# A hybrid decoder trunk on one core: the gathering tile's residual kept in the PEER accumulators, and 38 resident weight units in place of 31

## The chip, the core and the metric

One core of one Trainium2 chip runs the whole program: TensorE (PE), VectorE (DVE), ScalarE (ACT), GpSimd (POOL), SyncE (SP) and the core's 16 DMA engines. The metric is device microseconds (us) from the start to the end of the program, lower is better. Everything is float32.

## What is computed

The input is 256 tokens of 1024 numbers. Four layers follow each other: HGRN2, FoX attention, Mamba-2 SSD, HGRN2 again. In each, a token mixer and then a PEER layer are added to the residual; a last RMSNorm ends it. Cut to what matters here:

```python
for i in range(DEPTH):                       # 4 layers
    hn = rmsnorm(h, norm_mix[i])
    h = h + mixer[i % 3](hn, ...)            # hgrn2, fox, ssd
    ffn = peer_ffn(rmsnorm(h, norm_ffn[i]), peer_w_q[i], peer_keys[i], peer_u[i], peer_v[i])
    h = h + ffn
return rmsnorm(h, norm_final)

def peer_ffn(...):                           # 8 heads, 16384 experts of one neuron each
    q = (xb @ w_q).reshape(M, 8, 2, 128)
    s = einsum('mhcd,hckd->mhck', q, sub_keys)
    # top 16 of each half, top 16 of their 256 sums -> idx, gates
    u, v = take(u_tab, idx), take(v_tab, idx)
    act = gelu(einsum('md,mhkd->mhk', xb, u)) * gates
    return einsum('mhk,mhkd->md', act, v)
```

## The kernel before

**Tiles and stages.** The tokens are two tiles of 128. Layer and tile together make eight stages, s = 2 * layer + tile (`t`). In stage s the PEER experts of that stage are gathered while, as side work, the next stage's mixer, its second norm and its PEER queries are computed (`side`, L1332, calls `ready(s + 1, ...)`, L1302). Before the first stage the first tile's mixer runs alone (`lone`).

**The gather loop.** A stage has 64 steps (the loop at L1393). A step fetches two blocks of 128 rows of the expert table, one row of 8 KB (u and v) to each partition, so 1024 KB per fetch, by an indirect DMA that POOL issues (`fetch`, L1260). Eight buffers GB hold them, so up to eight fetches are out. DVE multiplies u with the tokens (`dot`, L1271), ACT makes gelu and gate and a diagonal weight (`spread`), and PE adds v times that weight to two PSUM accumulators `acc` (L1296), four products a step. A buffer is free for the next fetch when PE has read it. The accumulators are one pair of PSUM banks, reused by every stage.

**Residual.** Both tiles' residuals lie in SBUF, `h[:, t]`. When a stage's accumulators are complete, the first step of the next stage adds them to `h[:, t]` (`normed(..., alone=True)`, L444: two adds on DVE). Then come squares on ACT, root, scale, and the turned rows go into `xT`.

**Weights.** All weights come in units of 1024 KB, [128, 2048], in a fixed order (`stream`), once for each tile: a layer has 20 to 32 mixer units and 8 of the PEER queries. SP issues the loads (`loads`, L312). Most units pass through a ring of three (`raw`). A layer's first `EARLY` and last `LATE` units have a place of their own in the area `mix`; the second tile finds them there and loads nothing for them (L337). Before, that is 4 + 4 units for either HGRN2, 4 + 3 for FoX and 4 + 4 for SSD: 31 in all. What the mixer itself needs lies between (`middle`) or in the late units' places while the first tile runs, and in the early units' places while the second runs (`outer`). For the very first tile the list `order` (L296) writes out by hand which unit is loaded when, some of them into gather buffers that are still empty (`homes`).

**What sets the order.** Each engine runs its instructions in program order. The side work is cut into slots (`Plan`), and `products_` takes the next slot when its estimated cost so far is below a quota for the stage (`SIDE`, L40). SP's queue is in order too: a load that waits holds back all loads behind it. POOL's queue holds the gathers and four fills of a scratch tile.

Of the kernel before, what the change touches and what calls it, by code (L numbers as in the profile page):

```python
# [10 lines left out]
F32 = mybir.dt.float32  # L11
# [8 lines left out]
P = 128  # L20
# [90 lines left out]
def _layout(x, norm_mix, norm_ffn, norm_final, hgrn_lb_logits, hgrn_w_in, hgrn_gnorm, hgrn_w_out,  # L111
# [21 lines left out]
    def small(m):  # L133
# [5 lines left out]
    a["gn"] = np.ascontiguousarray(hgrn_gnorm)  # L139
    parts = [  # L140
        ("wf", small(w[:, 3072:3088])), ("wdt", small(w2[:, 6144:6176])),
# [24 lines left out]
def trunk(ctx: ExitStack, tc: tile.TileContext, d: dict, out: bass.AP):  # L166
# [15 lines left out]
    sizes = (("h", 2 * D), ("xT", D), ("XR", 2 * D), ("keys", UNIT), ("SS", 2048), ("mix", MIX),  # L182
# [6 lines left out]
    h = at_["h"].rearrange("p (t n) -> p t n", t=2)  # L189
# [56 lines left out]

    def middle(kind):
# [64 lines left out]
    def loads():  # L312

        while order:
# [4 lines left out]
            elif u == "x":  # L319
                nc.sync.dma_start(h[:, 1], d["x"][1])  # L320
# [123 lines left out]
    def normed(t, acc, row, xn, alone=False):  # L444
# [3 lines left out]
        r = st[:, 2:3]  # L448

        def add(e):  # L450
            tm(h[:, t, es[e]], acc[e], h[:, t, es[e]], op=OP.add)

        def square(e):
            act(xn[:, es[e]], h[:, t, es[e]], AF.Square, accum_out=st[:, e:e + 1])
# [5 lines left out]
        def scale():  # L460
            vec.reciprocal(r, r)
            for e in range(2):
                if last and t and e:
                    act(xn[:, es[e]], row[:, es[e]], AF.Copy, scale=r)
                elif last and t:
                    vec.tensor_scalar(xn[:, es[e]], row[:, es[e]], r, None, op0=OP.mult)
                elif last:
                    stt(xn[:, es[e]], h[:, t, es[e]], r, row[:, es[e]], op0=OP.mult, op1=OP.mult)
                if last:
                    nc.sync.dma_start(out[t * P:(t + 1) * P, es[e]], xn[:, es[e]])  # L470
                else:
                    vec.tensor_scalar(xn[:, es[e]], h[:, t, es[e]], r, None, op0=OP.mult)
# [5 lines left out]
        last = not isinstance(row, int)  # L478
        both = [lambda e=e: square(e) for e in range(2)]
        if acc is not None:  # L480
# [3 lines left out]
            else:  # L484
                both = [adds[0], both[0], adds[1], both[1]]
                if last and t:

                    for e in range(2):
                        both.insert(2 + 3 * e, lambda e=e: tm(row[:, es[e]], h[:, t, es[e]], row[:, es[e]], op=OP.mult))
                if lone[0] or last and t:  # L490
# [950 lines left out]
```

## Time and profile before

| what | us |
|---|---|
| median of 3 timed runs | 3188.8 (3187.67 to 3189.03) |
| the profiled execution, whole | 3185.7 |
| its span, first to last instruction | 3183.9 |
| PE busy in the span | 2470.2 (78%) |
| DVE busy | 2115.5 (66%) |
| ACT busy | 1351.3 (42%) |
| POOL busy | 1189.5 (37%) |
| time of the packets of the gathers' queue, as a share of 16 DMA engines | 81.8% |
| the same of the queue that loads weights | 17.3% |
| moved by DMA | 1303.02 MB |

The profile lists one execution. Its page has the busy time of each engine, the span in 40 slices, the DMA queues, and the costliest groups of instructions with the idle time ahead of them and what ended it. The trace behind it can be asked for any stretch of time. A float32 product stands in it as two records of PE. MB are millions of bytes.

### The profile page before, as it was taken

To read this page: it belongs to the slowest core of one execution; us is meant where nothing else is said; L and a number is where in the kernel's file an instruction comes from. 1 tells how busy PE (TensorE), PEld (TensorE's weight loads), DVE (VectorE), ACT (ScalarE), POOL (GpSimd) and SP (SyncE) were. 2 spreads that over 40 slices of the span, in tenths; PEclk is the share of its full clock that TensorE was granted. 3 is DMA by queue.
4 is the path that set the end of the run, shared out by engine and by line. 5 is a ranking of instruction groups with operands and counts; after the bars stand their busy time and mean duration, and the time that the engine had idled before them with its cause. 6 is when DMAs were issued, how large, how long until landed. Compare 5 with 4: busy or idle time off the path is not lost.

```text
span 3183.9 us, 30834 instructions
## 1 busy us (share of the span) xinstructions
PE 2470.2 (78%) x8610; PEld 1095.2 (34%) x8610; DVE 2115.5 (66%) x5584; ACT 1351.3 (42%) x3895; POOL 1189.5 (37%) x1032
## 2 busy tenths in 40 slices
PE   9888787877787876889878898778876877865655
PEld 4433333332333423344333443333332333332222
DVE  2576657675676756878567786476666767676764
ACT  3354324353344523577334773244433543333332
POOL 0243334343343424433334333244433433344443
PEclk9999898988899988999989998989988999898787
DMA  7899999999999999999999999999999999999997
GB/s 299 339 420 421 421 421 419 421 407 421 407 420 421 407 422 414 404 421 421 417 417 401 421 419 415 416 403 410 421 421 421 401 421 421 421 414 421 415 417 330
DMA packets 180025, 1303.02 MB, mean 409 GB/s; under 512 B 19984, under 2 KB 20368, under 8 KB 21520
## 3 DMA queue, kind: packets, MB, share of 16 engines
q0 software_dynamic: 147456, 1073.81, 81.8%
q1 hardware_dynamic: 32400, 227.24, 17.3%
q8 instruction: 72, 1.18, 0.2%
q14 instruction: 97, 0.79, 0.1%
HBM read 1299.92 MB, written 1.05 MB: 409 GB/s over the span
## 4 chain that ended last, share of the span: by engine, by line
DMA 58%; PE 14%; DVE 11%; issue 9%; ACT 4%; POOL 3%; POOLq 0%; DVEq 0%; ACTq 0%
DMA arena<-in_uv,ix 58%; DVE arena L204 8%; PE acc L1296 7%; PE pj L239 5%; POOL arena L1260 3%; PE ps L239 2%; ACT dots L217 1%; ACT L217 1%; DVE cs L204 1%; ACT dg L217 1%; PE ps L243 0%; DVE si L204 0%; ACT arena L217 0%; DVE sv L204 0%; DVE af L204 0%
## 5 line engine op out<-in xcount | busy, mean ns | idle before, releaser
L1260 POOL DMA_INDIRECT arena<-in_uv,ix x1024 | 1185.4, 1158 | 1968.6 <-PE acc L1296 1411.0
L204 DVE SCALAR_TENSOR_TENSOR arena<-arena 128x1024 f32<-128x1024 f32 (+3 forms) x1282 | 1322.1, 1048 | 878.5 <-DMA arena<-in_uv,ix 834.9
L1296 PE MATMUL acc<-arena,dg 128*64 128x512 f32 x4096 | 1285.2, 714 | 693.9 <-ACT dg L217 693.2
L1296 PEld LDWEIGHTS acc<-arena,dg 128*64 128x64 f32 x4096 | 466.0, 152 | 1326.4 <-ACT dg L217 1004.2
L217 ACT ACTIVATE dots<-dots 128x2 f32<-128x2 f32 x512 | 103.2, 202 | 1549.4 <-DVE arena L204 1549.3
L239 PE MATMUL pj<-raw,arena 128*128 128x512 f32 (+1 forms) x1368 | 635.5, 607 | 3.8 <-DMA raw<-in_ssm 2.8
L217 ACT ACT_TABLE_LOAD x325 | 417.0, 1283 | 6.8 <-DVE arena L204 0.8
L239 PEld LDWEIGHTS pj<-raw,arena 128*128 128x128 f32 x1368 | 249.8, 193 | 393.6 <-issue 377.4
L217 ACT ACTIVATE dg<-m,dots 128x64 f32<-128x64 f32 x1024 | 292.5, 333 | 0.0
L239 PE MATMUL pj<-arena 128*128 128x512 f32 x568 | 267.4, 616 | 0.3 <-DVE arena L204 0.3
L217 ACT ACTIVATE dots<-dots,gs 128x1 f32<-128x1 f32 x1024 | 245.6, 287 | 16.7
L239 PEld LDWEIGHTS pj<-arena 128*128 128x128 f32 x568 | 106.4, 197 | 162.5 <-issue 153.2
L239 PE MATMUL ps<-arena 128*128 128x128 f32 (+3 forms) x992 | 129.5, 286 | 1.1 <-ACT arena L1125 0.9
L239 PEld LDWEIGHTS ps<-arena 128*128 128x128 f32 (+2 forms) x992 | 102.7, 167 | 65.3 <-issue 39.0
L243 PEld LDWEIGHTS ps<-fst,arena 128*128 128x128 f32 x568 | 67.3, 147 | 85.5 <-issue 39.9
L243 PE MATMUL ps<-fst,arena 128*128 128x128 f32 x568 | 90.9, 288 | 4.5 <-ACT arena L1124 2.5
L217 ACT ACTIVATE arena<-arena 128x512 f32<-128x512 f32 (+3 forms) x132 | 67.7, 555 | 42.0 <-DVE arena L204 39.5
L204 DVE DVE_READ_ACCUMULATOR arena<-arena 128x1 f32 x1024 | 85.0, 83 | 0.0
L204 DVE FIND_INDEX8 si<-sv,arena 128x8 uint32<-128x128 f32 x256 | 69.9, 286 | 0.0
L239 PE MATMUL ps<-cst,arena 128*128 128x128 f32 (+3 forms) x288 | 67.0, 360 | 0.0
L204 DVE MAX8 sv<-arena 128x8 f32<-128x128 f32 x256 | 61.8, 283 | 5.7 <-ACT arena L1129 5.7
L217 ACT ACTIVATE arena<-ps 128x512 f32<-128x512 f32 (+3 forms) x114 | 43.7, 425 | 29.7 <-PE ps L239 29.0
(116 smaller groups left out, 1248.9 us busy)
## 6 DMA issues: line engine op xcount, KB each, us to landing
raw<-in_hg SPq DMA_DIRECT2D x57, 1024.0 KB, 9.4
raw<-in_ssm SPq DMA_DIRECT2D x56, 1024.0 KB, 9.4
raw<-in_wq SPq DMA_DIRECT2D x32, 1024.0 KB, 9.2
raw<-in_fox SPq DMA_DIRECT2D x24, 1024.0 KB, 9.2
arena<-in_wq SPq DMA_DIRECT2D x17, 1024.0 KB, 16.7
arena<-in_uv,ix POOLq DMA_INDIRECT x1024, 14.9
arena<-in_hg SPq DMA_DIRECT2D x15, 1024.0 KB, 14.1
arena<-in_keys SPq DMA_DIRECT2D x4, 1024.0 KB, 9.3
```

The lines of the kernel that those rows point to most:

```text
L204: return getattr(nc.vector, name)(o, *a, **k)
L217: nc.scalar.activation(o, i, f, **k)
L239: nc.tensor.matmul(o, w, m, start=start, stop=stop)
L243: nc.tensor.transpose(o, i, ident)
L1260: nc.gpsimd.indirect_dma_start(GB[n % NGB], None, d["uv"], bass.IndirectOffsetOnAxis(ap=got[s, hh][0][:, g, q:q + 1], axis=0))
L1296: nc.tensor.matmul(accs[s][e][g * 64:g * 64 + 64], dg[:, g], v, start=hh == 0 and q == 0, stop=hh == 7 and q == NQ - 1)
```

## The change

The residual of the tile whose experts are being gathered goes into that stage's accumulators. Its buffer is scratch from then on, and seven more weight units have places of their own.

- Two buffers `HB` of 1048 columns take the place of `h` (2 x 1024). In a stage one of them holds the residual that the side work works on (`hidden`), the other is its scratch (`spare_of`): the normed rows, HGRN2's `K`, SSD's convolution blocks and the PEER queries, which lay in `middle` before. They swap from stage to stage.
- `begin(s)` opens a stage's accumulators with two products of the identity and the tile's residual; the experts are then added to it. So when the stage ends the accumulators hold the new residual, and `normed(..., alone=True)` copies them out, one half on ACT and one on DVE, where it added both on DVE. The last norm of the second tile reads the accumulators themselves.
- `EARLY` and `LATE` become 5 + 5 for HGRN2, 4 + 5 for FoX and 4 + 5 for SSD: 10 + 9 + 9 + 10 = 38 units. HGRN2's `LF` and `SG`, and halves of FoX's keys and values, move into places of units (`outer`).
- In the hand-written order unit 23 has no gather buffer any more but its late place, and is loaded after the step "heads". The second tile's input is loaded after `begin(0)`, into the buffer that the first tile's residual has left.
- The projections `wf` and `wdt` (128 KB each) are loaded when their layer begins, not with the parameters. FoX's second tile multiplies with its two halves of keys in two products of 128 columns, not one of 256.
- The descriptor area of the gathers, `dynamic_dma_scratch_size`, goes from 4096 to 2048 bytes.

```diff
-EARLY = {"hg": 4, "fox": 4, "ssd": 4}
-LATE = {"hg": 4, "fox": 3, "ssd": 4}
-MIDDLE = {"hg": 4 * D + P, "fox": 64 + 8 * T + 3 * D + P, "ssd": 64 + 192 + 32 + 2 * D + 96 + T + 512 + 8 * 131}
+EARLY = {"hg": 5, "fox": 4, "ssd": 4}
+LATE = {"hg": 5, "fox": 5, "ssd": 5}
+MIDDLE = {"hg": D + P, "fox": 64 + 2 * D + P + T, "ssd": 64 + 192 + 32 + 2 * D + 96 + T + T}
+TURN = 8 * 131
...
-    sizes = (("h", 2 * D), ("xT", D), ("XR", 2 * D), ("keys", UNIT), ("SS", 2048), ("mix", MIX),
+    sizes = (("h0", TURN), ("h1", TURN), ("xT", D), ("XR", 2 * D), ("keys", UNIT), ("SS", 2048), ("mix", MIX),
...
+    def hidden(s):
+        return HB[(s - 1) % 2 if s else 0][:, 0:D]
+    def spare_of(s):
+        return HB[s % 2 if s else 1]
...
-    homes = {7: GB[0], 8: GB[1], 9: GB[2], 10: GB[3], 17: GB[0], 18: GB[1], 19: GB[2], 22: GB[5], 23: GB[6]}
-    order = [0, 1, 2, "rest", 3, 4, 5, 6, 7, 8, 9, 10, 11, 22, 12, 13, 23, 14, "x", 15, 16, 17, 20, 18, 21, 19, "keys",
-             "factors", 24, 25, "heads", 26, "states", 27]
+    homes = {7: GB[0], 8: GB[1], 9: GB[2], 10: GB[3], 17: GB[0], 18: GB[1], 19: GB[2], 22: GB[5]}
+    order = [0, 1, 2, "rest", 3, 4, 5, 6, 7, 8, 9, 10, 11, 22, 12, 13, 14, 15, 16, 17, 20, 18, 21, 19, "keys",
+             "factors", 24, 25, "heads", 23, 26, "states", 27]
...
-    def normed(t, acc, row, xn, alone=False):
+    def normed(h, t, acc, row, xn, alone=False):
...
+        src = [acc[e] if last and t else h[:, es[e]] for e in range(2)]
         def add(e):
-            tm(h[:, t, es[e]], acc[e], h[:, t, es[e]], op=OP.add)
+            if not alone:
+                tm(h[:, es[e]], acc[e], h[:, es[e]], op=OP.add)
+            elif e:
+                vec.tensor_copy(h[:, es[e]], acc[e])
+            else:
+                nc.scalar.copy(h[:, es[e]], acc[e])
...
+        if last and t:
+            for e in range(2):
+                both.insert(1 + 2 * e, lambda e=e: tm(row[:, es[e]], src[e], row[:, es[e]], op=OP.mult))
+            both.insert(2, lambda: act(spare, eps, AF.Sqrt))
...
-                mm(b[:, 0:nk * P], QT[ps, j], KT[ps, j, 0:nk * P], False, True)
+                for s in range(nk):
+                    mm(b[:, s * P:(s + 1) * P], QT[ps, j], KT[s][ps, j], False, s == nk - 1)
...
+    def begin(s):
+        accs[s] = [accp.tile([P, 512], F32, name="acc") for _ in range(2)]
+        for e in range(2):
+            nc.tensor.matmul(accs[s][e], ident, hidden(s)[:, e * 512:(e + 1) * 512], start=True, stop=False)
...
-        if hh == 0 and q == 0:
-            accs[s] = [accp.tile([P, 512], F32, name="acc") for _ in range(2)]
+        if s and hh == 0 and q == 0:
+            begin(s)
...
-                nc.tensor.matmul(accs[s][e][g * 64:g * 64 + 64], dg[:, g], v, start=hh == 0 and q == 0,
+                nc.tensor.matmul(accs[s][e][g * 64:g * 64 + 64], dg[:, g], v, start=False,
...
+        if not t and KIND[l] != "hg":
+            name = {"fox": "wf", "ssd": "wdt"}[KIND[l]]
+            nc.sync.dma_start(middle(KIND[l])(T), d[name])
...
     next(first)
+    begin(0)
+    nc.sync.dma_start(hidden(1), d["x"][1])
...
-    nc = bacc.Bacc("TRN2", target_bir_lowering=False, num_devices=1, dynamic_dma_scratch_size=4096)
+    nc = bacc.Bacc("TRN2", target_bir_lowering=False, num_devices=1, dynamic_dma_scratch_size=2048)
```

**SP, the loads from the first layer's second tile to the end of FoX's.** A row is a run of like loads. `raw` is the ring, `arena` a place of a unit (or a small table); `in_hg` and `in_fox` are mixer weights, `in_wq` those of the PEER queries. Before:

```order
L338 DMA raw<-in_hg 128x2048 x16
L338 DMA raw<-in_wq 128x2048 x4
L338 DMA arena<-in_fox 128x2048 x4
L338 DMA raw<-in_fox 128x2048 x3
L1309 DMA arena<-in_keys 128x2048
L338 DMA raw<-in_fox 128x2048 x9
L338 DMA raw<-in_wq 128x2048 x5
L338 DMA arena<-in_wq 128x2048 x3
L338 DMA raw<-in_fox 128x2048 x12
L338 DMA raw<-in_wq 128x2048 x5
```

After, where one more `raw<-in_hg` stands just ahead of the first row:

```order
L1388 DMA arena<-in_x 128x1024
L345 DMA raw<-in_hg 128x2048 x14
L345 DMA raw<-in_wq 128x2048 x3
L345 DMA arena<-in_fox 128x2048 x4
L345 DMA raw<-in_fox 128x2048 x3
L1329 DMA arena<-in_wf 128x256
L1332 DMA arena<-in_keys 128x2048
L345 DMA raw<-in_fox 128x2048 x9
L345 DMA raw<-in_wq 128x2048 x3
L345 DMA arena<-in_wq 128x2048 x5
L345 DMA raw<-in_fox 128x2048 x12
L345 DMA raw<-in_wq 128x2048 x3
```

The second tile of HGRN2 has 18 loads where it had 20, that of FoX 15 where it had 17. SSD's has 31 where it had 32, and the last HGRN2's 18 where it had 20. The second input tile's load stands behind the first of the second tile's ring loads; before, it stood among the first tile's units, ahead of its unit 15.

**PE, the seam between the first two stages.** `acc<-arena,dg` are the experts' products, four a step; `ps<-fst,arena 64x128` the 32 that repeat the next stage's tokens; `acc<-arena,fst` the products of `begin`. Before:

```order
L1296 MATMUL acc<-arena,dg 64x512 x28
L239 MATMUL ps<-fst,arena 64x128 x32
L1296 MATMUL acc<-arena,dg 64x512 x20
L243 MATMUL ps<-fst,arena 128x128 x8
L1296 MATMUL acc<-arena,dg 64x512 x4
```

After:

```order
L1316 MATMUL acc<-arena,dg 64x512 x28
L240 MATMUL ps<-fst,arena 64x128 x32
L1316 MATMUL acc<-arena,dg 64x512 x4
L1298 MATMUL acc<-arena,fst 128x512 x2
L1316 MATMUL acc<-arena,dg 64x512 x16
L244 MATMUL ps<-fst,arena 128x128 x8
L1316 MATMUL acc<-arena,dg 64x512 x4
```

The two products of `begin` come between the last step of the old stage and the first of the new. The same two stand at each of the seven seams, and once more at the start, behind the 32 repeating products of the first stage.

**DVE, the same seam.** `arena,dots<-arena` are the dots, two a step; `arena<-ps` copies repeated tokens. Before:

```order
L204 SCALAR_TENSOR_TENSOR arena,dots<-arena 128x1024 x4
L204 COPY arena<-ps 128x512
L204 SCALAR_TENSOR_TENSOR arena,dots<-arena 128x1024
L204 TENSOR_TENSOR arena<-acc,arena 128x512 x2
L204 SCALAR_TENSOR_TENSOR arena,dots<-arena 128x1024
L204 MAX sv<-arena 128x8 x2
```

After:

```order
L205 SCALAR_TENSOR_TENSOR arena,dots<-arena 128x1024 x4
L205 COPY arena<-ps 128x512
L205 SCALAR_TENSOR_TENSOR arena,dots<-arena 128x1024
L205 COPY arena<-acc 128x512
L205 SCALAR_TENSOR_TENSOR arena,dots<-arena 128x1024
L205 MAX sv<-arena 128x8 x2
```

Between the two dots of the new stage's first step stands one copy in place of two adds; the other half's copy stands on ACT, ahead of that step's gelu.

## Rows read from the trace of the kernel before

**Rows 1.** The page's second part, the span in 40 equal slices of 79.6 us: the busy share of the DMA engines in tenths, and what they moved.

```profile
DMA  7899999999999999999999999999999999999997
GB/s 299 339 420 421 421 421 419 421 407 421 407 420 421 407 422 414 404 421 421 417 417 401 421 419 415 416 403 410 421 421 421 401 421 421 421 414 421 415 417 330
```

**Rows 2.** Busy time of the engines in stretches: the lone start, the first PEER steps, and the eight gather stages (each from the first product into its accumulators to that of the next). Columns: stretch, its length, busy us and instructions of PE, its weight loads, DVE, ACT and POOL, PE's mean granted clock (1.00 is the higher of its two levels), the busy share of the DMA engines, GB/s.

```profile
0.00:117.00 117.00, 110.22 (x428) 59.47 (x428) 32.77 (x93) 37.81 (x71) 1.16 (x5) 1.00 0.78 306
117.00:160.00 43.00, 38.93 (x130) 18.44 (x130) 28.35 (x86) 15.64 (x45) 20.28 (x17) 0.93 0.90 355
134.00:518.00 384.00, 307.52 (x1057) 131.96 (x1057) 254.89 (x670) 157.81 (x461) 150.58 (x129) 0.92 1.01 416
518.00:892.00 374.00, 281.65 (x976) 123.04 (x976) 248.81 (x673) 149.92 (x471) 145.02 (x128) 0.87 1.01 415
892.00:1272.00 380.00, 287.90 (x1056) 131.55 (x1056) 253.81 (x677) 156.91 (x476) 148.01 (x129) 0.91 1.01 417
1272.00:1687.00 415.00, 345.59 (x1242) 157.36 (x1242) 299.14 (x821) 216.57 (x573) 152.00 (x128) 0.93 1.01 416
1687.00:2104.00 417.00, 346.31 (x1266) 158.23 (x1266) 298.43 (x811) 210.95 (x562) 146.89 (x129) 0.93 1.01 415
2104.00:2489.00 385.00, 296.37 (x1020) 128.15 (x1020) 253.57 (x655) 160.05 (x463) 153.44 (x130) 0.90 1.01 415
2489.00:2855.00 366.00, 289.42 (x1016) 124.68 (x1016) 253.98 (x655) 158.68 (x459) 150.28 (x130) 0.93 1.01 415
2855.00:3158.00 303.00, 177.41 (x482) 69.03 (x484) 200.82 (x492) 91.68 (x338) 133.86 (x121) 0.81 1.01 418
```

**Rows 3.** The page's fifth part, its costliest groups: busy us and mean ns of one, then the idle time before them and what ended most of it. The first is the gather's issue on POOL, the second the projections whose weights come through the ring.

```profile
L1260 POOL DMA_INDIRECT arena<-in_uv,ix x1024 | 1185.4, 1158 | 1968.6 <-PE acc L1296 1411.0
...
L239 PE MATMUL pj<-raw,arena 128*128 128x512 f32 (+1 forms) x1368 | 635.5, 607 | 3.8 <-DMA raw<-in_ssm 2.8
```

**Rows 4.** The page's third and sixth parts: the two DMA queues that carry data (packets, MB, share of the 16 engines' span), and two kinds of DMA issue (count, KB each, median us from issue to landing).

```profile
q0 software_dynamic: 147456, 1073.81, 81.8%
q1 hardware_dynamic: 32400, 227.24, 17.3%
...
raw<-in_hg SPq DMA_DIRECT2D x57, 1024.0 KB, 9.4
...
arena<-in_uv,ix POOLq DMA_INDIRECT x1024, 14.9
```

**Rows 5.** The seam between the first and second stage, instructions in order of time (start, us, engine, line, operation, idle before it and its releaser).

```profile
512.51 2.17 PE L1296 MATMUL acc<-arena,dg 128*64 128x512 f32 x8
...
514.51 1.28 DVE L204 TENSOR_TENSOR arena<-acc,arena 128x512 f32<-128x512 f32 x2
...
515.71 1.22 DVE L204 SCALAR_TENSOR_TENSOR arena<-arena 128x1024 f32<-128x1024 f32 x1
...
516.97 0.20 ACT L217 ACTIVATE dots<-dots 128x2 f32<-128x2 f32 x1 [3.80 <-DVE arena L204]
...
517.98 3.56 PE L1296 MATMUL acc<-arena,dg 128*64 128x512 f32 x8 [3.30 <-ACT dg L217]
```

**Rows 6.** Busy time of the engines in 25 us around the first of the seven seams and the three with the lowest rate, columns as in rows 2.

```profile
508.00:533.00 25.00, 15.79 (x103) 8.43 (x100) 18.39 (x52) 11.56 (x36) 11.50 (x11) 0.85 1.01 419
...
1262.00:1287.00 25.00, 15.90 (x107) 8.86 (x105) 19.00 (x56) 12.82 (x37) 12.60 (x10) 0.91 1.01 413
1677.00:1702.00 25.00, 15.97 (x105) 9.90 (x103) 19.90 (x56) 13.77 (x40) 12.06 (x10) 0.91 0.99 399
2094.00:2119.00 25.00, 16.77 (x107) 9.20 (x106) 19.30 (x56) 11.98 (x37) 11.88 (x11) 0.86 1.00 403
```

**Rows 7.** The start, instructions in order of time, from three pieces of the timeline put one after the other (the first is the warming of PE, three products in the code and six records in the trace).

```profile
1.49 5.37 PE L1278 MATMUL acc<-arena 128*128 128x512 f32 x6 [1.49 <-DVE arena L1345]
...
8.48 14.00 PE L239 MATMUL pj<-arena 128*128 128x512 f32 x32 [0.35 <-DVE arena L204]
...
62.00 0.43 SPq L320 DMA_DIRECT2D arena<-in_x  x1
...
98.73 11.75 SPq L338 DMA_DIRECT2D raw<-in_hg  x3
...
110.06 3.71 PE L239 MATMUL ps<-fst,arena 128*64 128x128 f32 x64
...
115.86 0.69 PE L243 MATMUL ps<-fst,arena 128*128 128x128 f32 x2 [2.09 <-ACT arena L1124]
...
117.16 1.08 POOL L1260 DMA_INDIRECT arena<-in_uv,ix  x1 [115.47 <-DVE ig L204]
...
118.03 12.78 PE L239 MATMUL pj<-arena 128*128 128x512 f32 x24
...
123.12 1.23 DVE L204 SCALAR_TENSOR_TENSOR arena<-arena 128x1024 f32<-128x1024 f32 x1 [5.40 <-DMA arena<-in_uv,ix]
...
134.23 2.17 PE L1296 MATMUL acc<-arena,dg 128*64 128x512 f32 x8 [3.00 <-ACT dg L217]
```

**Rows 8.** The end, instructions in order of time.

```profile
3173.88 1.94 PE L1296 MATMUL acc<-arena,dg 128*64 128x512 f32 x8
...
3175.03 0.69 DVE L204 TENSOR_TENSOR arena<-acc,arena 128x512 f32<-128x512 f32 x1 [3.33 <-PE acc L1296]
3175.75 0.63 ACT L217 ACTIVATE arena<-arena 128x512 f32<-128x512 f32 x1 [2.82 <-DVE arena L204]
```

More of the change, by code (lines that the diff above doesn't have):

```diff
@@ L448, in normed @@
         r = st[:, 2:3]
+        last = not isinstance(row, int)
+        src = [acc[e] if last and t else h[:, es[e]] for e in range(2)]
         def add(e):
-            tm(h[:, t, es[e]], acc[e], h[:, t, es[e]], op=OP.add)
+            if not alone:
[4 more added lines that the diff above has]
+                nc.scalar.copy(h[:, es[e]], acc[e])
         def square(e):
-            act(xn[:, es[e]], h[:, t, es[e]], AF.Square, accum_out=st[:, e:e + 1])
+            act(xn[:, es[e]], src[e], AF.Square, accum_out=st[:, e:e + 1])
         def root():
@@ L467, in scale @@
                 elif last:
-                    stt(xn[:, es[e]], h[:, t, es[e]], r, row[:, es[e]], op0=OP.mult, op1=OP.mult)
+                    stt(xn[:, es[e]], h[:, es[e]], r, row[:, es[e]], op0=OP.mult, op1=OP.mult)
                 if last:
@@ L476, in weighed @@
             tm(xT[:, c], b, weights[:, 8 * row + 4 * q:8 * row + 4 * q + 4].unsqueeze(2).to_broadcast([P, 4, P]), op=OP.mult)
-        last = not isinstance(row, int)
         both = [lambda e=e: square(e) for e in range(2)]
-        if acc is not None:
+        if last and t:
+            for e in range(2):
+                both.insert(1 + 2 * e, lambda e=e: tm(row[:, es[e]], src[e], row[:, es[e]], op=OP.mult))
+            both.insert(2, lambda: act(spare, eps, AF.Sqrt))
+        elif acc is not None:
             adds = [lambda e=e: add(e) for e in range(2)]
@@ L485, in normed @@
                 both = [adds[0], both[0], adds[1], both[1]]
[L486 to L490, printed above, removed]
+                if lone[0]:
                     both.insert(2, lambda: act(spare, eps, AF.Sqrt))
@@ L501, in hgrn @@
         al = middle("hg")
-        K, LF, SG, S = (al(D) for _ in range(4))
-        gn = al(P)
+        K, S, gn = carry["xn"], al(D), al(P)
+        al = outer("hg", t)
+        LF, SG = al(D), al(D)
         QT = SG.rearrange("p (h t) -> p h t", h=8)
@@ L741, in fox @@
         al = middle("fox")
-        al(D)
+        wf = al(T)
         LF = al(64).rearrange("p (t n) -> p t n", t=2)
-        KT = al(8 * T).rearrange("p (b t) -> p b t", b=8)
-        V = al(2 * D).rearrange("p (t n) -> p t n", t=2)
+        KT, V = [al(D)], [al(D)]
         gmem = al(P)
         al = outer("fox", t)
+        if t:
+            V.append(al(D))
+            KT.append(al(D))
+        KT = [k.rearrange("p (b t) -> p b t", b=8) for k in KT]
         QT = al(8 * P).rearrange("p (b t) -> p b t", b=8)
@@ L753, in fox @@
         nk = 1 + t
-        own = slice(t * P, (t + 1) * P)
         ub, sts, acc = {}, {}, []
@@ L776, in keys_turn @@
         def keys_turn(g):
-            turned(TM[1], lambda b: nc.scalar.copy(KT[:, 4 * g:4 * g + 4, own], b))
+            turned(TM[1], lambda b: nc.scalar.copy(KT[t][:, 4 * g:4 * g + 4], b))
         def scores(j):
@@ L887, in steps @@
             stt(DA, DT, -1.0, ea, op0=OP.mult, op1=OP.mult)
-        gate = small_proj("wdt", "dtb", steps, RR)
+        gate = small_proj(wdt, "dtb", steps, RR)
         def suffix():
@@ L1094, in queries @@
         ub = {}
-        al = middle(KIND[l])
-        QB = al(512)
-        QT = al(512).rearrange("p (g t) -> p g t", g=4)
+        QB = spare_of(s)[:, 0:512]
+        QT = spare_of(s)[:, 512:D].rearrange("p (g t) -> p g t", g=4)
         def evac(g):
@@ L1314, in ready @@
             free(("late", l))
-        norm = normed(t, carry["acc"], DEPTH + l, xn)
+        norm = normed(h, t, carry["acc"], DEPTH + l, xn)
         if lone[0]:
@@ L1423, in trunk @@
             pass
-    for _ in normed(1, accs.pop(STAGES - 1), mix[:, 0:D], mix[:, 2 * D:3 * D]):
+    for _ in normed(None, 1, accs.pop(STAGES - 1), mix[:, 0:D], mix[:, 2 * D:3 * D]):
         pass
```

36 lines of the change are left out of this document (16 added, 20 removed).

## The prediction

> **What bounds the kernel now.** I read the slices of the span first. From the third slice to the last but one the DMA engines are at 9 tenths and move 401 to 422 GB/s; only the first two slices (299 and 339) and the last (330) are well below [rows 1]. That is a ceiling, not chance: the eight stages run at 415 to 418 GB/s whatever they compute [rows 2]. The stage from 1687 has 417 us and the one from 2489 has 366 us, both at 415 GB/s, so 173.1 MB and 151.9 MB: 51 us for 21.2 MB, 2.41 us for each MB. The time of a stage is its bytes. The compute engines follow: PE is busy for 307.52 of 384 us in the first stage (80%) and 346.31 of 417 in the fullest (83%), and even there the rate is 415 [rows 2].
>
> Then I read who waits. POOL's idle time ahead of a gather mostly ends with PE's products, which free the buffer [rows 3]; but a gather takes 14.9 us from issue to landing [rows 4], and at 421 GB/s its 1.049 MB is 2.49 us of transfer, so some six gathers' worth of data is ahead of it: the DMA engines have work in reserve while POOL waits. PE waits for ring weights 3.8 us in all [rows 3], so the loads are no latency problem; they cost bytes in the DMA engines. Their queue has 17.3% of the engines' time, the gathers' 81.8% [rows 4].
>
> The start is another regime. Until the first gather (117.16) PE is busy 110.22 of 117 us at 306 GB/s, and until 160 us the rate is 355 [rows 2, 7]. There bytes are free and PE's chain counts.
>
> **The change part by part.** *Seven loads fewer.* The order of SP shows them: two each in the second tile of HGRN2, FoX and the last HGRN2, one in SSD's. 7 x 1024 KB are 7.34 MB. At the ceiling of 421 GB/s [rows 1] that is 17.4 us; by the stages' mean of 416 it is 17.6; by packet time, 99.1% of 3183.9 us for 1301.05 MB, 2.425 us each MB, 17.8 [rows 4]. I take 17.4. All seven are loads of stages that run close to the ceiling (those from 134, 892, 1687 and 2489). One would be a ring load from about 100 us, in the slow start, but the ring stays three loads deep, so the load that disappears is the last of the row, not the first.
>
> The Trainium skill speaks against that price: its page "DMA: Bandwidth & Descriptors", section "Where 436 GB/s comes from", has HBM bind transfers to the core at about 358 GB/s, by which the saving would be an estimated 20.5 us. The trace disagrees: 420 GB/s and more stand in slice after slice [rows 1]. The 17.4 holds without it.
>
> *Small tables.* `wf` and `wdt`, 131 KB each, leave the start and go into the saturated part: 0.262 MB, +0.6 us. They are needed behind the next tile's norm and 1024 KB loads land in 9.4 us [rows 4], so I cost no wait.
>
> *The second input tile* (0.524 MB) was issued at 62.00, and now behind `begin(0)` [rows 7]. SP holds the ring loads behind it, two of 1.049 MB, which were issued by 110.5 and now go at about 115.5. So 2.6 MB move to the first gathers, up to 6.2 us of transfer. But from 117 to 160 us the rate is 355, which leaves 43 us x 66 GB/s = 2.8 MB unused [rows 2], because the queries' products hold PE for 12.78 us from 118.03 and the first expert product comes at 134.23, while its first dot could start at 123.12 [rows 7]. I take 0; if half of the room is already spoken for, +3 us.
>
> *begin.* One such product is two records of 0.44 us (14.00 / 32), or 0.90 in the slowest row (5.37 / 6) [rows 7]: two products are 1.75 to 3.6 us. At the start they fall into PE's gap of 2.09 us ahead of 115.86 [rows 7]: 0. At a seam PE has finished the old stage at 514.68 and waits 3.30 us for ACT until 517.98 [rows 5]. The accumulators come free while it waits: DVE's two adds (1.28 us from 514.51) become one copy on DVE, taken as half of that, and one on ACT, which has nothing else until 516.97. The first product can start at about 514.7, the second at 515.3, and both end by 516.5. DVE's next dot starts 0.6 us earlier, so the chain of dot, gelu and product gains 0.6 us at each of seven seams, if PE keeps up. Around the seams the rate is 399 to 419 [rows 6], the reserve feeds the DMA engines through most of it; I take 0, with 4 us (7 x 0.6) as the gain at best.
>
> *The other PE work.* Eight begins are 14 us of 2470 and FoX's 16 additional products some 14 more at the same price; PE would be busy 82% of a shortened first stage, still under the 83% that runs at 415 [rows 2]. Cover: 18% idle PE. 0.
>
> *The end.* Behind the last product an add (0.69 us, 3175.03) stood ahead of the first square (3175.75) on the path to the output [rows 8]. The square now reads the accumulators: -0.7 us.
>
> *The smaller descriptor area* costs nothing as long as POOL need not wait for an old gather; the trace has no row for that, bounds below.
>
> Sum: -17.4 + 0.6 - 0.7 = -17.5 us. The profiled execution had 3185.7 (a span of 3183.9 and 1.8 around it), which makes 3168.2; its own time was 3.1 under the median, and against the median, 3188.8, I expect **3171.3 us**. From the bounds: +3 at the start and a fifth of the saving lost to steps in which PE is late give 3178; -0.4, 4 at the seams give 3167.
>
> **The rivals.** *Saved bytes, but an engine takes the bound.* If the four shortened stages hung on PE for half of what they save, 8.7 us come back: 3180.0. For it: PE is busy for 80% there, and the rate dips to 401 to 407 in single slices. Against it: the stage from 2855 has next to no weights, so its gathers come faster than they ever will elsewhere, and it runs at 418; the fullest stage still has 415 [rows 2].
>
> *The seams get longer.* If both products wait for the end of both reads and PE runs them at the slow price, they go from about 515.8 to 519.4, 1.4 us past 517.98 [rows 5, 7]; seven times 1.4 is 9.8, and the time is 3181. It would need an empty reserve, too; the poorest seam has 399 GB/s, the first 419 [rows 6].
>
> *Slower: the descriptor area throttles the gathers.* With room for too few, POOL would wait for an old gather to land before it can write the next. The one gather with nothing ahead took 5.96 us, 117.16 to 123.12 [rows 7]; with two at a time that is 2.98 us each, 0.49 above 2.49, and 1024 gathers lose 502 us. With three to five at a time the rate holds on average, but without a reserve each stage would run like the poorest seam, 399 for 416 GB/s [rows 2, 6]: 4.3% of the 3041 us from 134 to 3175, +130 us, so 3301. It decides from fewer than six at a time, the number that the landing time shows. Against it: with the area of before POOL's issues average 1158 ns, and what it waits for is PE [rows 3]; nothing hints that it is near its limit.
>
> On this rival the Trainium skill, "DMA: Bandwidth & Descriptors", sections "Terms" and "The descriptor swizzle", has descriptors of 16 bytes and nine to an engine for a 1 MiB transfer; an estimate from that page is 2048 / 16 = 128, or 14 gathers, more than the eight buffers ask for. The nine agree with the trace, 147456 packets / 1024 gathers / 16 engines [rows 4]; the area's room no run here shows.
>
> That the loads don't go away is no rival: they are gone from SP's order.
>
> **How the numbers follow.** My forecast, 3171.3 with its own range 3167 to 3178, gets 0.82; an engine that takes the bound (about 3180) 0.08; longer seams (about 3181) 0.06; the throttle 0.04. The range is 3165 to 3180: the forecast's with 2 us at the lower end for clock and order effects on the start's chain, and half of the first rival's; 0.14 is left out. A measurement of this kernel tells about 0.2% from no change, 6.4 us, so faster means under 3182.4. The forecast, three quarters of the first rival and two thirds of the second are faster: 0.92. Same: 0.04. Slower: the throttle, 0.04.
>
> **What would show it.** The weights' queue carries about 7.3 MB less, and the stages from 134, 892 and 2489 are some 5 us shorter, the one from 1687 some 2, at the same 415 to 418 GB/s; the other four keep their length. PE's wait ahead of a stage's first expert product shrinks by the 1.75 us of `begin`, and that product does not come later after the seam's last dot. The first gather is still issued at about 117, and the last square starts with no add ahead of it. If the shortened stages show a lower rate at the old length, the first rival holds; if POOL's idle time ends with DMA, or its issues get longer, the third does. I am wrong altogether if PE's chain in the start moves by more than a few us, because there every microsecond counts fully.

## The result, and the profile after

The changed kernel takes 3170.4 us (median of 5 runs, 3169.8 to 3174.4), the kernel before, beside it, 3187.7 (3186.3 to 3189.0): a ratio of 0.9949, 95% interval 0.9935 to 0.9964, or 17.3 us less. The forecast was 17.5 us less and 3171.3. The profiled execution's span is 3172.0, 3173.7 with what lies around it.

The page's second and third parts after: busy share of the DMA engines and GB/s in 40 slices, now of 79.3 us, and the two queues (packets, MB, share).

```profile
DMA  6899999999999999999999999999999999999998
GB/s 271 359 417 421 421 421 422 421 416 422 412 411 421 393 421 413 417 420 419 421 411 407 421 421 407 411 411 409 421 421 399 406 422 421 400 418 421 420 417 337
...
q0 software_dynamic: 147456, 1073.81, 82.2%
q1 hardware_dynamic: 31680, 219.90, 16.8%
```

The ceiling is the one of [rows 1], the gathers' queue is the one of [rows 4], and the weights' queue carries 227.24 - 219.90 = 7.34 MB less: the seven loads. The two small tables have gone from the start into the same queue and don't change its sum.

The stretches that answer to [rows 2], columns as there:

```profile
0.00:118.00 118.00, 111.33 (x432) 60.02 (x432) 32.53 (x92) 37.80 (x71) 1.15 (x5) 1.00 0.69 279
118.00:160.00 42.00, 37.48 (x120) 16.97 (x120) 25.21 (x74) 15.75 (x45) 16.73 (x16) 0.92 1.01 416
133.00:515.00 382.00, 304.64 (x1060) 130.42 (x1060) 258.97 (x684) 158.75 (x461) 153.41 (x129) 0.93 1.01 420
515.00:889.00 374.00, 277.44 (x980) 122.94 (x980) 247.03 (x670) 150.93 (x472) 140.00 (x128) 0.89 1.01 418
889.00:1265.00 376.00, 286.55 (x1093) 130.11 (x1094) 253.25 (x680) 158.74 (x478) 146.31 (x129) 0.90 1.00 412
1265.00:1678.00 413.00, 340.91 (x1248) 154.73 (x1247) 299.31 (x822) 217.91 (x574) 146.89 (x128) 0.94 1.01 418
1678.00:2097.00 419.00, 348.30 (x1270) 158.72 (x1268) 297.98 (x807) 211.65 (x561) 146.38 (x128) 0.91 1.01 414
2097.00:2481.00 384.00, 296.48 (x1024) 127.79 (x1024) 252.83 (x652) 160.26 (x464) 150.07 (x130) 0.90 1.00 412
2481.00:2845.00 364.00, 291.02 (x1020) 124.15 (x1020) 252.73 (x652) 158.76 (x459) 148.27 (x129) 0.92 1.01 413
2845.00:3147.00 302.00, 177.52 (x481) 68.53 (x481) 201.32 (x491) 93.32 (x341) 130.43 (x120) 0.80 1.01 420
```

Read length times rate, not length alone. The stages still run at 412 to 420 GB/s. Their MB, before and after: first 384 x 416 = 159.7 and 382 x 420 = 160.4; third 158.5 and 154.9; fourth 172.6 and 172.6; fifth 173.1 and 173.5; sixth 159.8 and 158.2; seventh 151.9 and 150.3. So the first stage keeps its bytes. The first two rows tell why: the start carried 117 x 306 = 35.8 MB and now 118 x 279 = 32.9; the 42 us behind it run at 416 and carry 17.5 MB where 43 us at 355 carried 15.3. By the queues' packets the first stage's weights do fall, from 26.2 to 24.25 MB, but 2.6 MB more of gathers land in it, since only 3.6 MB of them were moved ahead of its first product, 6.1 before.

The groups that answer to [rows 3], busy us and mean ns, then the idle time ahead:

```profile
L1274 POOL DMA_INDIRECT arena<-in_uv,ix x1024 | 1167.4, 1140 | 1976.1 <-PE acc L1316 1352.9
...
L240 PE MATMUL pj<-raw,arena 128*128 128x512 f32 (+1 forms) x1264 | 586.3, 606 | 3.1 <-DVE arena L205 2.1
```

POOL's issue is no longer than before (1140 ns, 1158 then), what it waits for is still PE, and PE hardly waits for ring weights.

The first seam after, in order of time, which answers to [rows 5]:

```profile
510.00 2.17 PE L1316 MATMUL acc<-arena,dg 128*64 128x512 f32 x8
...
511.34 0.58 ACT L465 COPY arena<-acc 128x512 f32<-128x512 f32 x1 [0.69 <-PE acc L1316]
...
512.09 1.98 PE L1298 MATMUL acc<-arena,fst 128*128 128x512 f32 x4
...
512.20 0.69 DVE L205 COPY arena<-acc 128x512 f32<-128x512 f32 x1
512.81 1.22 DVE L205 SCALAR_TENSOR_TENSOR arena<-arena 128x1024 f32<-128x1024 f32 x1
...
515.07 2.17 PE L1316 MATMUL acc<-arena,dg 128*64 128x512 f32 x8 [0.99 <-ACT dg L218]
```

The products of `begin` wait for the copies and lie where PE waited 3.30 us before; 0.99 is left. The new stage's first expert product comes 1.04 us after the end of the seam's last dot (512.81 + 1.22 = 514.03), as before (1.05, from 516.93 to 517.98). From the old stage's last product to that first one it is 2.90 us, 3.30 before.

### The profile page after: what moved, and what is told of

It reads as the page before. It is cut to its first block, busy times and chain, and to the rows that moved or that the text cites. A ratio compares the mean times of both kernels' runs of the same rounds, so it can differ in the third digit from the quotient of the medians.

```text
span 3172.0 us, 30948 instructions
## 1 busy us (share of the span) xinstructions
PE 2458.5 (78%) x8674; PEld 1088.0 (34%) x8674; DVE 2110.0 (67%) x5575; ACT 1359.4 (43%) x3904; POOL 1171.5 (37%) x1032
## 3 DMA queue, kind: packets, MB, share of 16 engines
q1 hardware_dynamic: 31680, 219.90, 16.8%
HBM read 1292.58 MB, written 1.05 MB: 408 GB/s over the span
## 4 chain that ended last, share of the span: by engine, by line
DMA 54%; PE 19%; DVE 12%; issue 8%; ACT 4%; POOL 3%; POOLq 0%; SPq 0%; DVEq 0%; ACTq 0%
DMA arena<-in_uv,ix 54%; PE acc L1316 9%; DVE arena L205 9%; PE pj L240 6%; POOL arena L1274 3%; PE ps L240 3%; ACT dots L218 2%; DVE cs L205 1%; ACT L218 1%; ACT dg L218 1%; PE ps L244 1%; DVE si L205 0%; DVE ti L205 0%; ACT arena L218 0%; DVE af L205 0%
## 5 line engine op out<-in xcount | busy, mean ns | idle before, releaser
L1274 POOL DMA_INDIRECT arena<-in_uv,ix x1024 | 1167.4, 1140 | 1976.1 <-PE acc L1316 1352.9
L205 DVE SCALAR_TENSOR_TENSOR arena<-arena 128x1024 f32<-128x1024 f32 (+3 forms) x1282 | 1320.7, 1048 | 845.2 <-DMA arena<-in_uv,ix 804.4
L1316 PE MATMUL acc<-arena,dg 128*64 128x512 f32 x4096 | 1262.0, 705 | 693.8 <-ACT dg L218 679.3
L1316 PEld LDWEIGHTS acc<-arena,dg 128*64 128x64 f32 x4096 | 453.4, 152 | 1316.3 <-ACT dg L218 964.2
L240 PE MATMUL pj<-raw,arena 128*128 128x512 f32 (+1 forms) x1264 | 586.3, 606 | 3.1 <-DVE arena L205 2.1
L240 PEld LDWEIGHTS pj<-raw,arena 128*128 128x128 f32 x1264 | 230.7, 193 | 365.8 <-issue 345.4
L240 PE MATMUL pj<-arena 128*128 128x512 f32 x672 | 310.6, 607 | 1.8 <-DMA arena<-in_hg 1.8
L240 PEld LDWEIGHTS pj<-arena 128*128 128x128 f32 x672 | 122.9, 192 | 186.0 <-issue 175.3
L240 PE MATMUL ps<-arena 128*128 128x128 f32 (+6 forms) x1088 | 135.4, 281 | 1.1 <-ACT arena L1139 0.9
L240 PEld LDWEIGHTS ps<-arena 128*128 128x128 f32 (+3 forms) x1088 | 110.2, 168 | 67.7 <-issue 45.5
```

Of the source, the lines that this page charges most:

```text
L205: return getattr(nc.vector, name)(o, *a, **k)
L240: nc.tensor.matmul(o, w, m, start=start, stop=stop)
L1274: nc.gpsimd.indirect_dma_start(GB[n % NGB], None, d["uv"], bass.IndirectOffsetOnAxis(ap=got[s, hh][0][:, g, q:q + 1], axis=0))
L1316: nc.tensor.matmul(accs[s][e][g * 64:g * 64 + 64], dg[:, g], v, start=False, stop=hh == 7 and q == NQ - 1)
```

## The experiments

Each was run beside the kernel before on the same chip, five rounds (three for the area of 512 bytes); differences are from its median there. The intervals reach 3 to 6 us either way, so a difference of one or two microseconds is not settled by times.

**The changed kernel again**, without an edit. 

> The changed kernel once more, to learn its own spread: its first five runs stood in two groups, near 3170 and near 3174 us. By the theory that the gain is the time of seven loads (7.34 MB at some 421 GB/s) the median stays at 3170 to 3174, 14 to 18 us under the kernel before. By the rival that only a lucky order of transfers made it, the time goes up to 3176 or more in part of the runs. A second profile should show whether the stages from 134 and 2489 us are shortened by about 5 us each, as the bytes say, or by less than 2, as the first profile has it.

3167.1 us against 3184.7: 0.9942 (0.9929 to 0.9956), 17.5 us less. In this execution the stages from 134, 892 and 2489 are 0.7, 5.8 and 4.2 us shorter than before and the one from 1687 is 0.6 longer; in the first they were 1.6, 4.5 and 1.7 shorter and 2.5 longer. So the length of a single stage is uncertain by some 2 us. The next three shared its chip and its runs of the kernel before.

**The seven units loaded again**, each into the place where it already lies; all else is the changed kernel.

```diff
+AGAIN = {"hg": (4, 23), "fox": (19, 20), "ssd": (35,)}
...
-                if not t or places[u][3] is None:
+                if not t or places[u][3] is None or places[u][2] in AGAIN[KIND[places[u][1]]]:
```

> The changed kernel, but the seven units that the second tiles no longer load are loaded again, each into its own resident place; all else of the change stays (residual in the accumulators, buffers in turn, smaller descriptor area). By the theory that the gain is bytes, all of it goes: 17 us more than the changed kernel, 3186 to 3189, level with the kernel before within 3 us. By the rival that the seams, the shorter end and the new order of the start carry half of it, the time is 3176 to 3180, clearly under the kernel before.

3184.0 us, 0.9995 (0.9986 to 1.0004): 16.9 above the changed kernel. The third part of its page has the bytes back:

```profile
q1 hardware_dynamic: 32688, 227.24, 17.3%
```

**The seven left out of the kernel before.** The second tiles multiply with the layer's last resident unit in their place.

```diff
+LEFT = {"hg": (4, 23), "fox": (19, 20), "ssd": (35,)}
...
+                if t and i_(u) in LEFT[KIND[places[u][1]]]:
+                    raws[u] = last_place(u), True
+                    order.pop()
+                    continue
```

> The kernel before with nothing of the change but its saving: the second tiles of the four layers leave out the loads of the same seven units and multiply with the layer's last resident unit in their place, so those projections use wrong weights; all instructions of PE, DVE, ACT and POOL stay. By the theory of bytes the time falls by the whole 17 us, to 3169 to 3173. By the rival that it needs the other parts, it falls by half or less, to 3179 or more.

3167.9 us, 0.9944 (0.9931 to 0.9958): 16.8 less. The seven loads make the whole difference from either side. All the rest of the change together, moving the residual included, is the 0.7 us that the kernel with the loads put back is under the one before (4.5 less to 1.3 more): none that can be measured. Nearly all that is moved here goes in transfers of 1024 KB, so these runs do not tell bytes from the number of such transfers.

**The smaller descriptor area alone**, in the kernel before.

```diff
-dynamic_dma_scratch_size=4096)
+dynamic_dma_scratch_size=2048)
```

> The kernel before with only the descriptor area of the gathers changed, from 4096 to 2048 bytes. By the theory that POOL never waits for room, no change: 3186 to 3189, POOL's mean issue near 1158 ns. By the rival that the smaller area throttles the gathers a little and eats part of the saving, 3 us or more slower.

3183.5 us, 0.9996 (0.9987 to 1.0005): nothing that can be measured.

**`begin` three times at each seam.** The first two rounds of products are overwritten by the third.

```diff
-            nc.tensor.matmul(accs[s][e], ident, hidden(s)[:, e * 512:(e + 1) * 512], start=True, stop=False)
+            for k in range(3 if s else 1):
+                nc.tensor.matmul(accs[s][e], ident, hidden(s)[:, e * 512:(e + 1) * 512], start=True, stop=s > 0 and k < 2)
```

> The changed kernel with the products of begin made three times at each of the seven seams (six in place of two, the first four overwritten, the result unchanged). That is 3.5 us more of PE ahead of a stage's first expert product at the higher clock, 24.5 us over seven seams. By the theory that PE waits there for ACT anyway and the gathers in reserve feed the DMA engines, at most 5 us more than the changed kernel. By the rival that a seam is on the path, 15 to 25 us more.

3167.5 us, 0.9945 (0.9931 to 0.9958), where the next kernel below, the changed one with an area of 1024 bytes, has 3166.9 on the same chip. PE at its first seam:

```profile
512.05 2.17 PE L1317 MATMUL acc<-arena,dg 128*64 128x512 f32 x8
514.14 5.42 PE L1299 MATMUL acc<-arena,fst 128*128 128x512 f32 x12
519.49 1.08 PE L1317 MATMUL acc<-arena,dg 128*64 128x512 f32 x4
```

The seam is 5.3 us from the old stage's last product to the new one's first, 2.4 longer than the changed kernel's. The other six are as long. Seven times 2.4 would be 17 us, and 0.6 is seen, less than the noise of some 4. So most of that length costs nothing; a gain there of a few tenths would not be seen either.

**The area at 1024 bytes, and at 512**, in the changed kernel (`dynamic_dma_scratch_size`, nothing else).

> The changed kernel with a descriptor area of 1024 bytes in place of 2048. By the estimate that a gather takes nine entries of 16 bytes, seven gathers fit where eight buffers ask; only three or four are out when POOL issues the next, so no change within 3 us. By the rival that the area is already near its limit at 2048, slower by 10 us or more.

> The changed kernel with a descriptor area of 512 bytes: by the same estimate three gathers fit. By the price in the prediction the rate then holds on average but the reserve is gone, 130 us slower, and POOL's waits or issues get longer; if the area bounds less than I think, no change; with a round trip of 6 us for three gathers of 2.5 us, more than 500 us slower is not expected.

1024 bytes: 3166.9 us, 0.9949 (0.9935 to 0.9962), no change from 2048. 512 bytes: 3415.8 us, 1.0729 (1.0709 to 1.0749), 249 us above the run with 1024. The rates in slices, POOL's group and the gather's row of the DMA issues (median us from issue to landing) with 512:

```profile
GB/s 279 347 371 392 408 388 362 402 370 409 363 374 392 381 398 382 394 400 396 414 364 383 394 400 412 373 362 394 391 408 370 381 387 389 370 352 356 373 366 320
...
L1274 POOL DMA_INDIRECT arena<-in_uv,ix x1024 | 1549.6, 1513 | 1846.2 <-issue 730.8
...
arena<-in_uv,ix POOLq DMA_INDIRECT x1024, 8.7
```

With 1024:

```profile
arena<-in_uv,ix POOLq DMA_INDIRECT x1024, 13.9
```

POOL's issue grows from 1140 to 1513 ns, and the cause named for the largest part of its idle time turns from PE into none that the profile shows (730.8 of 1846.2 us). A gather every 3.2 us (some 3290 us for 1024) that lands after 8.7 means 2.7 in flight; with 1024 bytes it is 13.9 / 2.96 = 4.7, before the change 14.9 / 2.97 = 5.0. On the size from which an area throttles, an estimate from the Trainium skill ("DMA: Bandwidth & Descriptors", "Terms" and "The descriptor swizzle": 16 bytes a descriptor, nine to an engine for such a transfer) is 7.1 gathers in 1024 bytes and 3.6 in 512; the traces agree with it, 4.7 in flight unhindered and 2.7 held back. The start shows the limit itself, since all buffers are empty there. POOL with 512 bytes:

```profile
118.06 1.08 POOL L1274 DMA_INDIRECT arena<-in_uv,ix  x1 [116.36 <-DVE ig L205]
119.44 0.93 POOL L1274 DMA_INDIRECT arena<-in_uv,ix  x1 [0.30 <-issue]
120.68 0.94 POOL L1274 DMA_INDIRECT arena<-in_uv,ix  x1 [0.30 <-issue]
128.55 1.64 POOL L1274 DMA_INDIRECT arena<-in_uv,ix  x1 [6.93 <-issue]
```

With 1024, the seventh and the eighth:

```profile
126.19 0.94 POOL L1274 DMA_INDIRECT arena<-in_uv,ix  x1 [0.30 <-issue]
128.91 1.63 POOL L1274 DMA_INDIRECT arena<-in_uv,ix  x1 [1.79 <-DMA arena<-in_uv,ix]
```

Three are issued in a row with 512 bytes, seven with 1024, and all eight with 2048 (the eighth at 127.25). In both kernels the next one is issued 0.41 us after the first dot starts (128.14 and 128.50), so when the first gather has landed.

**Fourteen more loads left out**, in the changed kernel; the layer's last resident unit stands in for them, as above.

```diff
+LEFT = {"hg": (5, 6, 21, 22), "fox": (16, 17, 18), "ssd": (32, 33, 34)}
```

> The changed kernel with fourteen more loads left out in the second tiles (four each in the two HGRN2 layers, three each in FoX and SSD; those projections use a resident unit, so wrong weights). 14.68 MB at 421 GB/s are 34.9 us. By the theory that bytes bound, 31 to 36 us less than the changed kernel. By the rival that PE takes the bound when its share passes 85% or so, half of it or less, 17 us, and the rate in the stages from 134 and 2489 falls under 410 GB/s.

3136.5 us, 0.9849 (0.9835 to 0.9862): 30.5 below the run with 1024 bytes, 2.2 us for each load, and just short of the 31 to 36 expected. Its queue, and its stage from 1659, in which SSD's second tile is computed:

```profile
q1 hardware_dynamic: 29664, 205.22, 15.9%
...
1659.00:2076.00 417.00, 346.94 (x1270) 156.51 (x1268) 298.08 (x809) 211.38 (x562) 146.05 (x128) 0.91 1.00 407
```

Bytes still set most of the time, but 14.68 MB at 416 GB/s would be 35 us. In this one execution the stage from 1659 is short of its share: it keeps the length of the changed kernel's (417 and 419 us) with 3.1 MB less of weights, at 407 GB/s in place of 414; the others run at 413 to 421. What holds the gathers back in it, and whether that is the other 5 us, isn't settled.

**Where room for four more units could come from.** Two buffers of 1024 KB could be given up: one of the ring's three, or one of the eight gather buffers. Either makes 42 resident units, and four loads fewer (215.70 MB in the weights' queue, not 219.90). A third kernel has the smaller ring with the 38 units, so that its price is seen alone. In both with two ring places, two units of the start's order go to empty gather buffers.

```diff
-NRAW = 3
+NRAW = 2
-EARLY = {"hg": 5, "fox": 4, "ssd": 4}
+EARLY = {"hg": 6, "fox": 5, "ssd": 5}
-    homes = {7: GB[0], 8: GB[1], 9: GB[2], 10: GB[3], 17: GB[0], 18: GB[1], 19: GB[2], 22: GB[5]}
+    homes = {7: GB[0], 8: GB[1], 9: GB[2], 10: GB[3], 17: GB[0], 18: GB[1], 19: GB[2], 22: GB[5], 12: GB[6], 13: GB[7]}
```

> After with a ring of two units in place of three; the room goes to four more resident units (42; two more for HGRN2, one each for FoX and SSD, four or five loads fewer in the second tiles). Theory (only bytes count): 4 to 5 loads at 2.1 to 2.5 us are 8 to 12 us, so 3156 to 3161 where the changed kernel has 3166 to 3170, queue q1 about 5 MB less. Rival (the ring's depth was what kept the loads no latency problem): a 1 MB load lands 9.4 us after its issue, and a ring unit is used up about every 8 us, so with two places PE waits a few us at many of the some 135 ring loads, with the experts' products queued behind it; if a fourth of that goes past the reserve, +50 us and more, PE's idle time ahead of the ring's products rises from 3 us to 100 or more, and ends with DMA.

> After with a ring of two units and the same 38 resident units: the ring's cost alone. Theory (only bytes count, PE's waits lie beside the transfers): within 2 us of the changed kernel, 3165 to 3172, though PE waits longer for weights. Rival (depth counts): slower by what the run with 42 units is short of its saving, some 10 to 60 us.

The one with fewer gather buffers has `NGB` 7 and the same `EARLY`.

> After with seven gather buffers in place of eight; the room goes to the same 42 resident units. Theory (only bytes count, since seven buffers still leave the DMA engines with work): 3156 to 3161, the stages at the same 415 to 418 GB/s. Rival (the reserve counts): six gathers' worth of transfer lies ahead of each in the changed kernel; with one buffer less it is five, and the stages' rate falls at the seams and in steps in which PE is late; 0.5 to 1.5% of 3040 us are +15 to +45, so 3172 to 3205, GB/s under 415 in the stages.

Ring of two, 42 units: 3165.1 us, 0.9940 (0.9927 to 0.9954), 19.0 less than before. Ring of two, 38 units: 3175.3, 0.9972 (0.9961 to 0.9983), 8.9 less. Seven buffers, 42 units: 3176.0, 0.9974 (0.9962 to 0.9985), 8.2 less. The four loads are worth 3175.3 - 3165.1 = 10.2 us, 2.5 each, like the seven. The ring's third place is worth 17.5 - 8.9 = 8.6 us. Each of these is a difference of two, known to some 5 us. So the theory that only bytes count missed both times with the smaller ring (3156 to 3161 and 3165 to 3172 expected), and its rival was too dear (50 us and more with 42 units, 10 to 60 with 38, and 100 us of PE's waits). PE's waits with two places and 38 units (us in total, times, longest):

```profile
PE pj L240 <- DMA raw<-in_ssm: 27.5, 13, 3.4
...
PE pj L240 <- DMA raw<-in_wq: 15.2, 7, 3.0
PE pj L240 <- DMA raw<-in_fox: 4.2, 2, 2.5
```

PE waits 47 us for ring weights, and most of that stays hidden. The eighth buffer is worth most: the seven-buffer kernel is short by 17.5 + 10.2 - 8.2 = 19.5 us. The same 3000 us of the changed kernel, and of the one with seven buffers:

```profile
140.00:3140.00 3000.00, 2312.05 (x8152) 1013.22 (x8150) 2055.07 (x5431) 1306.93 (x3786) 1157.47 (x1014) 0.90 1.01 416
```

```profile
140.00:3140.00 3000.00, 2326.18 (x8149) 1015.38 (x8149) 2055.93 (x5430) 1306.02 (x3786) 1154.10 (x1013) 0.89 1.01 414
```

2 of 416 GB/s are 14 us of 3000, give or take 7 for the rounding: the reserve of the DMA engines is thin enough that one gather less of it shows. So the rival of that run held in its price and in the rate, but not in the place: 25 us around each seam of the seven-buffer kernel move 419 to 422 GB/s, so the rate falls elsewhere in the stages. Of the two ways the buffer's loses (8.2 us less in place of 17.5, with intervals apart), and the ring's comes out level with the changed kernel (19.0 and 17.5).

**The start of the kernel with the smaller ring mended.** Unit 14 goes to GB[4]: `homes` gets `14: GB[4]`.

> The kernel with a ring of two and 42 resident units, and in the lone start unit 14 goes to the empty gather buffer GB[4] and not through the ring. There a ring of two makes SP hold unit 17 behind the ring's loads, PE waits 3.0 us for two units with places of their own, and the first gather comes 2.7 us later than in the changed kernel (121.1 for 118.4). Theory (the start counts fully): first gather at 118.5 to 119.5 and 2 us off, 17.5 + 10 - 6 = 21.5 us under the kernel before. Rival (the start's delay is made up later, or something else holds it): as without the edit, 19.0 under the kernel before, within 1.

3162.8 us, 0.9935 (0.9921 to 0.9949): 22.3 less than before, 21.5 expected. Its first gather:

```profile
119.12 1.08 POOL L1274 DMA_INDIRECT arena<-in_uv,ix  x1 [117.43 <-DVE ig L205]
```

It comes 2.0 us earlier than without the edit (121.12), as the theory had it. This is the lowest median of the kernels that leave nothing out, some 5 us under the changed kernel by these differences. But its interval overlaps that of the changed kernel and that of the kernel without the edit (19.0 less), so neither order is settled, nor is it shown that the start counts fully.

## Why the prediction was right, step by step

**The bound and the main term.** DMA bytes set the time, and seven loads are 17 us: shown from both sides (+16.9 put back, -16.8 taken out), forecast 17.4. That the whole came out 0.2 us from the forecast (17.3 for 17.5) is closer than the runs can tell (11.5 to 20.7 us less), and so in part luck. The small terms, +0.6 and -0.7, cancel in the sum; no run shows the +0.6 by itself, and together with all else but the loads they are the unmeasurable -0.7 us.

**Where in the program the bytes fall** was wrong for two stages. "The stages from 134, 892 and 2489 are some 5 us shorter, the one from 1687 some 2" came out at about 2, 4, 2, and 2 longer, and in the second execution at 1, 6, 4, and 1 longer. The third and the seventh fit the bytes within that spread. The first saved its two loads but took in the gathers that the start no longer carried, which the prediction moved there itself and left out of this sign. For the stage from 1687, I gave each saved load to the stage that computes with it. But the last HGRN2's fifth early unit, a ring load of the stage from 2104 before, is now loaded with its other early units in the stage from 1687, and takes the place of SSD's saved load there: by its packets, the weights' queue has 38.9 MB in that stage before and after, and 25.2 and 24.1 in the next. The sum over the stages doesn't care.

**The start.** The step that took 0 for 2.6 MB moved behind `begin(0)` held within about 1 us: the room that it counted on, 355 GB/s from 117 to 160, is used (416 now); the first dot starts 5.2 us later than before (128.31 and 123.12), but the first expert product comes at 132.90, not later than 134.23; and by 160 us the gathers' queue has moved 14.8 MB, 15.25 before. The first gather was said to stay at 117 and is issued at 118.42. That is not the change's doing; the first weights landed later in this execution. The start after, in order of time:

```profile
9.76 2.81 PE L240 MATMUL pj<-arena 128*128 128x512 f32 x6 [1.76 <-DMA arena<-in_hg]
...
114.96 1.98 PE L1298 MATMUL acc<-arena,fst 128*128 128x512 f32 x4
...
118.42 1.08 POOL L1274 DMA_INDIRECT arena<-in_uv,ix  x1 [116.73 <-DVE ig L205]
...
128.31 1.23 DVE L205 SCALAR_TENSOR_TENSOR arena<-arena 128x1024 f32<-128x1024 f32 x1 [9.33 <-DMA arena<-in_uv,ix]
```

Before, PE's projections started at 8.48 [rows 7], 1.28 us earlier, and the gather 1.26 earlier. The kernel before with the area of 2048 bytes shows such a delay with the old order, and no loss in time:

```profile
9.55 2.81 PE L239 MATMUL pj<-arena 128*128 128x512 f32 x6 [1.50 <-DMA arena<-in_hg]
...
118.21 1.08 POOL L1260 DMA_INDIRECT arena<-in_uv,ix  x1 [116.52 <-DVE ig L204]
```

Nor is it the area: the kernel before without the seven loads has the old order and 4096 bytes, and waits as well:

```profile
10.03 2.90 PE L240 MATMUL pj<-arena 128*128 128x512 f32 x3 [1.92 <-DMA arena<-in_hg]
```

**The seams.** PE's wait took `begin` in, as argued; the 0.6 us of gain at each is 0.4 and is not seen in the time, as the value 0 had it. The rival of longer seams fell in its first half (they are shorter), and its price was wrong too: 2.4 us longer at each, more than its 1.4, costs nothing that is seen, where 1.4 was to cost 9.8.

**The end.** -0.7 is the term that was mis-sized, though it is small. The second execution of the changed kernel, in order of time:

```profile
3157.43 1.94 PE L1316 MATMUL acc<-arena,dg 128*64 128x512 f32 x8
...
3158.58 0.60 ACT L218 ACTIVATE arena<-acc 128x512 f32<-128x512 f32 x1 [2.31 <-PE acc L1316]
...
3160.69 0.58 ACT L218 ACTIVATE arena<-acc 128x512 f32<-128x512 f32 x1
...
3161.39 0.69 DVE L205 TENSOR_TENSOR arena<-acc,arena 128x512 f32<-128x512 f32 x1 [1.40 <-ACT arena L218]
3162.00 0.15 DVE L205 TENSOR_TENSOR st<-st 128x1 f32<-128x1 f32 x1
...
3163.22 0.81 SPq L484 DMA_DIRECT2D out<-arena  x2
```

Before, the output was issued at:

```profile
3179.91 0.81 SPq L470 DMA_DIRECT2D out<-arena  x2
```

The first square comes 1.15 us after the start of the last products, where it was 1.87 [rows 8]: there are the 0.7. But DVE's multiplication of the second half now reads the same accumulator as the second square, starts only after it (its wait ends with ACT, and the two share nothing else), and stands ahead of the sum of the squares (3162.00), which it holds up by some 0.6. The output is issued 5.79 us after the last products' start, 6.03 before: 0.24 is kept. In the first execution it is 6.00 (3162.11 to 3168.11), with products that took 2.17 us and not 1.94: so hardly anything is kept there.

**An engine that takes the bound**: not here. The medians with the loads put back and left out are within 0.6 us of the bytes' 17.4, where this rival would have given back 8.7. One of its signs shows in part: the stage from 892 has 412 GB/s in both executions, 417 before, but it is shorter with its bytes (4.5 and 5.8 us). With fourteen more loads gone it is 2.2 us each in place of 2.5, and one stage is down to 407 GB/s; that such an effect takes the 0.3 isn't shown, nor ruled out.

**The throttle** stayed away at 2048 bytes, as weighed, but its point and its price were wrong. "From fewer than six at a time" took 14.9 us over 2.49 us for the number in flight, as if gathers had the DMA engines to themselves; a gather comes every 2.97 us, so it is 5.0, and 4.7 cost nothing. And without a reserve the rate is not the poorest seam's 399: with 2.7 in flight it is 384 from 140 to 3380 us, down to 352 in a slice, and the price was 249 us, not 130. "Three to five at a time" lumped together what costs nothing (4.7 on the mean) and what costs 8% (at most three).

## What to carry to other kernels

Where a profile shows one transfer rate in stages of different work, price an edit by bytes over that rate, and check it by putting the bytes back; here a unit of 1024 KB kept on chip was worth 2.4 to 2.5 us, while 2.4 us more at each of seven seams cost nothing that was seen. Before on-chip room is spent on fewer bytes, price what held it before: the third place of the weight ring was worth 8.6 us, the eighth gather buffer 19.5, and four more resident units 10.2, each known to some 5. For the number of transfers in flight divide the landing time by the time between two of them, not by the time of one alone.

## What was not expected of the hardware

- The indirect gathers ran equally fast with descriptor areas of 4096, 2048 and 1024 bytes, and 7.9% slower with 512 (3415.8 against 3166.9 us): no cost down to 1024, and a large one at the next halving. From an empty start three gathers go out in a row with 512 bytes and seven with 1024.
- One gather buffer of eight is worth some 0.6% of the time (19.5 us), though POOL's issues on the page wait for freed buffers two thirds of its idle time in either case and the busy share of the DMA engines stays at 9 tenths in all slices but the first two and the last.
- 47 us of PE's waits for weights at the head of its queue cost some 8.6 us in all, and 2.4 of these may be in the start (first gather at 120.85, not 118.42).
